# Layer 1's input projection reordered: gate strips ahead of the latents, and the normalised latents kept on chip

## The chip, the cores and the metric

The kernel runs on one NeuronCore of one Trainium2 chip. Five engines work side by side, each through an instruction list of its own that is fixed when the kernel is built: PE (TensorE, matmuls and transposes), DVE (VectorE), ACT (ScalarE), POOL (GpSimd) and SP (SyncE, which here only issues DMAs). They wait for each other through semaphores. The metric is device time in microseconds (us) of one execution. Before the change the median of three executions is 1457.54 us, from 1457.47 to 1457.69.

## The reference, cut to what matters

A two-layer encoder trunk on 1024 tokens of width 1024 in float32. Layer 0 is differential attention, layer 1 multi-head latent attention (MLA), and a last RMSNorm closes it. The change lies in the projections of layer 1:

```python
proj = h @ w_in
q_a, c_kv, k_pe, z = split(proj, [384, 640, 704])         # 384, 256, 64 and 1024 columns
q = (_rmsnorm(q_a, q_a_norm_g) @ w_q_b).reshape(b, s, 8, 192)
q_nope, q_pe = q[..., :128], _rope(q[..., 128:], positions)
k_pe = _rope(k_pe[:, :, None, :], positions)[:, :, 0]
kv = (_rmsnorm(c_kv, kv_a_norm_g) @ w_kv_b).reshape(b, s, 8, 256)
k_nope, v = kv[..., :128], kv[..., 128:]
sc = (einsum('bqhd,bkhd->bhqk', q_nope, k_nope) + einsum('bqhr,bkr->bhqk', q_pe, k_pe)) * 192 ** -0.5
o = einsum('bhqk,bkhd->bqhd', softmax(sc), v)
out = (o * silu(z)) @ w_out
```

So q_a (three strips of 128 columns) and c_kv (two strips) each need an RMS norm over their own columns before anything can be projected out of them. The gate z (eight strips) and k_pe (one) need no norm.

## The kernel before, in words

**Split arithmetic.** Every float32 operand of a matmul is held as two tiles, a rounded high half and a low half (what rounding left over), and each product is three matmuls of 128x128 by 128x512: high·high, high·low, low·high (`mm3`, L177 to L180; the weight's half is named first). A weight tile that a DMA brought to "wraw" is split by ACT (wh, L223) and POOL (wl, L224).

**Strips.** All activations are kept transposed: 128 columns of a projection on the partitions, tokens along the row, in two halves of 512 tokens. A half strip of h takes 8 steps of `mm3`, 24 matmuls. `w_s1` numbers layer 1's strips: 0 is k_pe, 1 to 3 the q latents, 4 and 5 the kv latents, 6 and 7 the gate of head 0 and 1. The gates of heads 2 to 7 are made two at a time by `z_pair` (L1408 to L1435), a Strassen-like scheme: 7 products of 12 matmuls instead of 8 for two strips by two halves. Products 2, 3, 1 and 4 use sums and differences of quarters of h, built on DVE and ACT by `combos` (L1233 to L1260); the weights of a pair are combined on DVE in `z_weights` (L1383 to L1386: zs, then a21, a11 and a12 in their "zraw" tiles), then split. The product with TC[2] is the third of a pair and uses the combination a11 of L1385.

**Norms.** `lora` (L1276) takes a group of latent strips. ACT copies each half strip to "craw" (L1282) and squares it; DVE adds the squares up in "csum" (L1290). When the last strip of the group is through, four matmuls with a column of ones sum over the columns (cps, L1295), DVE and POOL make the inverse root (c_w, L1297; rq_y, L165), and since it is then one number per token lying on the wrong axis, it goes out to DRAM (bc_d, L401) and comes back spread over all partitions (bc_s, L403). DVE scales craw by it (L1304), ACT rounds the high half (c_h, L1308), POOL takes the low one (L1309), and both halves are stored to DRAM in "cS" (L1315, L1316). These steps stand in a list that `run_norms` empties one stage at a time, at the fifth step of a half strip (`NORM_AT = 4`).

**Order of the stage.** Second token half of h is made from x (transposes trh, L482; the scaled copies h1f); strips 0 and 1 for the first half run meanwhile. Then strip 0 and 1 second half, 2, 3, 4, 5, the gates 6 and 7, three `z_pair`s, in the last of which 20 DMAs of 256 KB bring the latents back (`load_ck`, L1458 to L1462). Then eight value tiles of heads 0 to 3 one after the other (`v1_tile`, L1448: 6 matmuls, a split by ACT and DVE at L356, a store of 512 KB to "vS" at L358). Then the stream of q and k strips: strip qr (rope part of two heads), kn and qn of head 0, with the value tiles of heads 4 to 7 set between them by `V1_AT = (3, 2)`: 3 tiles after 6 steps, 2 tiles after the remaining ones of 16, 3 after the first scores. Rope needs its rows swapped, which four DMAs do (rp_sw, L319), a DVE add (rp_r, L329), and DMAs that stack the halves (qpa, L350; qpb, L351).

**What sets the order.** The program text. Loops over matmul steps call `side.tick()`, which runs one entry of a queue of small tasks; the list of each engine follows from the text and from a scheduler that keeps an engine's list in an order by readiness, save where the text pins it (`keep_in_program_order`). SP's list holds every DMA of the stage, loads, stores and norm rows alike, in one queue: a DMA whose data is late holds back those behind it. Tiles come from pools of fixed size ("zraw" 6, "wraw" 2, "u" 20), and a tile's next user waits for its last reader.

## Time and profile before

| what | number |
|---|---|
| median of three executions | 1457.54 us |
| the profiled execution, its own time | 1457.54 us |
| its span in the trace | 1457.5 us |
| PE, matmul instructions | 7388 |
| first half strip of layer 1 begins | about 782 us |
| the three pairs | 898.5 to 957.2 us |
| first scores of layer 1 | 994.96 us |
| DMA traffic of the whole | 213.70 MB |

The span and the execution's own time differ by under 0.1 us, so what is found in the trace can be set against the time as it is. A row of the profile names its line (L1295 is line 1295), its engine, the operation and its tiles (out<-in). In a timeline row the two numbers ahead are the start and the duration in us, and the bracket behind tells how long the engine had been idle and what ended that. A window row gives for each engine the busy time and the number of instructions, then the clock that PE was granted (1.00 is full), the share of the DMA engines that was busy, and what they moved. A PE that waits shows as missing busy time; a PE with a lowered clock shows as busy, but its matmuls are longer.

### The profile page before, as it was taken

The numbers are of one execution on the slowest core, as the hardware profiler recorded it, in microseconds if no ns is written. First come the engines' busy times: TensorE is split into PE (matmuls) and PEld (weight loads), VectorE is DVE, ScalarE is ACT, GpSimd is POOL, SyncE is SP. The second block draws the span as 40 slices with busy tenths as digits, with TensorE's granted clock in tenths as the row PEclk, the third lists the DMA queues.
The fourth block names the chain that finished last, engine by engine and source line by source line (L and its number), as shares of the span: only waits on it lengthen the run. The fifth ranks groups of instructions, "written<-read, shape, count | busy, mean of one in ns | idle before, by whom it ended". The sixth has DMA issues, their size and how long they took to land. (4 is left out here: it accounts for less than half of the span.)

```text
span 1457.5 us, 20649 instructions
## 1 busy us (share of the span) xinstructions
PE 1396.9 (96%) x7388; PEld 1166.4 (80%) x7388; DVE 917.9 (63%) x1362; ACT 727.8 (50%) x1287; POOL 627.6 (43%) x493
## 2 busy tenths in 40 slices
PE   5999999999999999998999879989999999999997
PEld 4778788888888887886787768867888888888886
DVE  6656777767777767687355964544666555555355
ACT  5622365656566665565343433334455554545342
POOL 4416164656465555543641455422141331412572
PEclk9999999999999999999999989999999999999999
DMA  9787723333332424237743145398443432336563
GB/s 329 228 252 237 245 67 99 85 99 87 102 93 82 114 68 117 59 87 261 253 144 123 44 152 173 107 289 211 146 125 123 118 104 65 110 97 215 181 234 141
DMA packets 135527, 213.70 MB, mean 147 GB/s; under 512 B 19072, under 2 KB 56064, under 8 KB 135424
## 3 DMA queue, kind: packets, MB, share of 16 engines
q1 hardware_dynamic: 135424, 212.38, 47.7%
q8 instruction: 58, 0.95, 0.3%
q14 instruction: 45, 0.37, 0.1%
HBM read 137.92 MB, written 50.80 MB: 129 GB/s over the span
## 5 line engine op out<-in xcount | busy, mean ns | idle before, releaser
L378 ACT CAST pth<-tr 128x512 fp32r<-128x512 f32 x256 | 150.3, 587 | 281.7 <-PE tr L376 280.0
L393 DVE TENSOR_REDUCE nm<-s 128x1 f32<-128x1024 f32 x192 | 234.0, 1219 | 76.8 <-PE s L767 65.7
L379 DVE TENSOR_TENSOR ptl<-tr,pth 128x512 fp32r<-128x512 f32 x256 | 176.1, 688 | 140.1 <-ACT pth L378 139.6
L224 POOL TENSOR_TENSOR wl<-wraw,wh 128x512 fp32r<-128x512 f32 (+2 forms) x81 | 106.8, 1321 | 210.7 <-ACT wh L223 202.2
L395 ACT ACTIVATE e<-s,nm 128x1024 f32<-128x1024 f32 x128 | 143.7, 1122 | 31.8 <-DVE nm L393 26.2
L376 PE MATMUL tr<-ident,e 128*128 128x128 f32 x1024 | 154.6, 273 | 2.2 <-DVE ptl L379 1.9
L376 PEld LDWEIGHTS tr<-ident,e 128*128 128x128 f32 x1024 | 121.5, 140 | 42.9 <-DVE ptl L379 19.4
L178 PE MATMUL acc<-h0h,wh 128*128 128x512 f32 x360 | 150.8, 419 | 3.6 <-DVE v_hl L356 3.1
L178 PE MATMUL pv<-pth,vt 128*128 128x256 f32 x512 | 147.2, 287 | 0.0
L179 PE MATMUL pv<-ptl,vt 128*128 128x256 f32 x512 | 145.6, 284 | 0.0
L180 PE MATMUL pv<-pth,vt 128*128 128x256 f32 x512 | 144.6, 282 | 0.0
L180 PE MATMUL acc<-h0h,wl 128*128 128x512 f32 x360 | 142.8, 397 | 0.3 <-POOL wl L224 0.3
L179 PE MATMUL acc<-h0l,wh 128*128 128x512 f32 x360 | 142.1, 395 | 0.0
L1007 POOL TENSOR_TENSOR wol<-wor,woh 128x512 fp32r<-128x512 f32 x64 | 85.6, 1360 | 83.3 <-ACT woh L1006 78.9
L179 PEld LDWEIGHTS pv<-ptl,vt 128*128 128x128 f32 x512 | 97.7, 191 | 2.6
L178 PEld LDWEIGHTS pv<-pth,vt 128*128 128x128 f32 x512 | 97.6, 191 | 2.8 <-ACT pth L378 0.2
L180 PEld LDWEIGHTS pv<-pth,vt 128*128 128x128 f32 x512 | 97.7, 191 | 0.1
L320 POOL TENSOR_TENSOR rp_r<-rp_raw,cosT 128x512 f32<-128x512 f32 x38 | 49.8, 1311 | 94.9 <-ACT rp_raw L315 51.7
L325 POOL TENSOR_TENSOR rp_sw<-rp_sw,sinT 128x512 f32<-128x512 f32 x42 | 55.7, 1326 | 77.8 <-DMA rp_sw<-rp_raw 73.0
L767 PE MATMUL s<-ks,qa 128*128 128x512 f32 x256 | 82.0, 402 | 3.0 <-DVE e L775 2.7
L775 DVE SCALAR_TENSOR_TENSOR e<-s,z,e 128x1024 f32<-128x1024 f32 x64 | 82.1, 1283 | 2.1
L767 PE MATMUL s<-ks,qb 128*128 128x512 f32 x256 | 80.9, 395 | 0.0
(590 smaller groups left out, 3365.2 us busy)
## 6 DMA issues: line engine op xcount, KB each, us to landing
ada<-in_ada_ss SPq DMA_DIRECT2D x32, 512.0 KB, 5.8
wraw<-in_w_s SPq DMA_DIRECT2D x64, 256.0 KB, 2.9
vS<-v_hl SPq DMA_DIRECT2D x32, 512.0 KB, 5.3
vt<-vS SPq DMA_DIRECT2D x32, 512.0 KB, 3.9
wor<-in_w_out SPq DMA_DIRECT2D x64, 256.0 KB, 4.0
rp_sw<-rp_raw SPq DMA_DIRECT2D x168, 64.0 KB, 2.0
bc_s<-bc_d SPq DMA_DIRECT2D x34, 256.0 KB, 4.4
oS<-bc_s SPq DMA_DIRECT2D x30, 256.0 KB, 3.0
```

Of the source, the lines that this page charges most:

```text
L178: PE.matmul(psum, ah, bh, start=first, stop=False)
L179: PE.matmul(psum, ah, bl, start=False, stop=False)
L180: PE.matmul(psum, al, bh, start=False, stop=last)
L224: sub = (V if pair_of else G).tensor_sub(l_[:, :n], raw[:, :n], f32v(h_[:, :n]))
L376: PE.transpose(tr[:, j, :], p[:, kt * P : (kt + 1) * P], ident)
L378: mk["S"] = S.copy(pth[kh][:, :, dst], tr).ins
L379: mk["V"] = V.tensor_sub(ptl[kh][:, :, dst], tr, f32v(pth[kh][:, :, dst])).ins
L393: mk["V"] = V.reduce_max(nm, s_ps, axis=AX.X, negate=True).ins
L395: mk["S"] = S.activation(e, s_ps, AF.Exp, bias=nm, scale=1.0, accum_out=zs).ins
L767: PE.matmul(s_ps[:, kc * HF : (kc + 1) * HF], src[:, c, ql], KS[h][kc][:, c, :], start=fst, stop=not fst)
L775: combined.append(V.scalar_tensor_tensor(out=e0, in0=e1, scalar=z1[:, 0:1], in1=e0, op0=ALU.mult, op1=ALU.add).ins)
L1007: in_turn(G.tensor_sub(lo, raw, f32v(hi)))
```

## The change

The strips are taken in another order. After k_pe come the gates 6 and 7, then the kv latents 4 and 5, then the three pairs; the q latents 1 to 3 come last, as the first three items of the stream that used to begin with qr. The norm of the kv latents runs inside the first pair: `z_pair` calls `late_z`, which now empties one stage of the norm list at each of its three points. The norm of the q latents runs behind the value tiles: eight tiles of heads 0 to 3 are set at every fourth step of the last two q strips and the kn strip (after 16 steps), and those of heads 4 to 7 between kn, qr and qn of head 0 by `V1_AT = ((2, 4), (3, 6), (0, 6), (1, 0))`: number of tiles, then steps of the stream. Two tiles are left for after the first scores.

The normalised latents no longer go to DRAM: cS, its 20 stores and its 20 loads are gone. Their high and low halves go to tiles that stay (pool "ck", 8 tiles, for c_kv, and "u" for q_a). The low half is taken by DVE now (POOL before), in a stage of its own, `split`, one stage behind the scaling.

Smaller edits: the copies of k_pe go from DVE to ACT; the h1f copies of the second token half go from DVE to ACT (`act=gi == 1`); two empty ticks (`G_LATE`) stand ahead of the second half's transposes; the combinations follow each other at 4 ticks (5 before); the value tiles' buffers of layer 1 are 5 (`VB`, 3 before); the size of a scratch area for DMAs is set when the kernel is built.

```diff
-V1_AT = (3, 2)
+QA_V = 16
+V1_AT = ((2, 4), (3, 6), (0, 6), (1, 0))
+G_LATE = 2
-VB = (2, 3)
+VB = (2, 5)
@@ group0
-            h_chunk(1, fulls, k, h1[k][gi], p3x, V, f32=h1f[k] if gi else None)
-        if gi == 0:
-            side.add(*[None] * G_WAIT)
+            h_chunk(1, fulls, k, h1[k][gi], p3x, V, act=gi == 1, f32=h1f[k] if gi else None)
+        side.add(*[None] * (G_LATE if gi else G_WAIT))
...
-            side.add(lambda: w4.append(strip1(0)), None, lambda: w4.append(strip1(1, h1p)))
+            side.add(lambda: w4.append(strip1(0)), None, lambda: w4.append(strip1(6, h1p)))
@@ lora
-            def rest():
+            def scale():
                 for i in range(n):
                     t = craw[i][half]
                     tc.keep_in_program_order(V.scalar_tensor_tensor(
...
-                    hi = pl.tile([P, HF], F32R, name="c_h", tag=tag, bufs=6)
-                    S.copy(hi, t)
-                    G.tensor_sub(t.bitcast(F32R), t, f32v(hi))
-                    his.append(hi)
-                norms.append(store)
-            def store():
-                for i in range(n):
-                    SP.dma_start(cS[dst + i, half, 0], f32v(his[i]))
-                    SP.dma_start(cS[dst + i, half, 1], craw[i][half])
+                norms.append(split)
+            def split():
+                for i in range(n):
+                    t = craw[i][half]
+                    dst[i][half] = hi, lo = part(), part()
+                    S.copy(hi, t)
+                    V.tensor_sub(lo, t, f32v(hi))
...
-    lora((1, 2, 3), 0, qag, QL, w4[1], first_halves)
-    lora((4, 5), 3, kvg, KVL)
-    for h in range(2):
-        w = strip1(6 + h)
+    half_and_norm(w4[0], 1, lambda acc: side.q.insert(8, kp_half(1, acc)))
+    half_and_norm(w4[1], 1, z_put(0, 1))
+    w = strip1(7)
+    for half in range(2):
+        half_and_norm(w, half, z_put(1, half))
+    for i in range(2):
+        w = strip1(4 + i)
+        for half in range(2):
+            half_and_norm(w, half, lambda acc: ckput(i, half, acc))
...
     def late_z(i):
-        if i == 0:
-            load_ck(CK, 3, [(k, half) for half in range(2) for k in range(2)])
-        if i == 2:
-            load_wk(0)
-            load_ck(CQ, 0, [(i, half) for half in range(2) for i in range(3)])
+        run_norms()
-    z_pair(1)
+    z_pair(1, late_z)
     load_wk(1)
-    z_pair(2)
-    z_pair(3, late_z)
-    for tt in range(NT):
-        v1_tile(tt, 0, p4)
+    z_pair(2, late_z)
+    z_pair(3, late_q)
+    cqput = lora(3, CQ, qag, QL, lambda: ut("cqr", dt=F32), lambda: ut("cq"), 1)
...
-    items, steps1 = [], []
+    items = [(lambda i=i: fetch_strip([A["w_s1"][1 + i, f] for f in range(2)], [4, 4]), h1, lambda acc, half, i=i: cqput(i, half, acc)) for i in range(3)]
...
-    stream1.step(6)
+    stream1.step(QA_V)
+    for tt in range(NT):
+        v1_tile(tt, 0, p4)
+        stream1.step(4)
+        if tt % 2:
+            run_norms()
-    for n, steps in zip(V1_AT, (steps1[0] - 6, 0)):
+    for n, steps in V1_AT:
         for tt in v1_left[:n]:
             v1_tile(tt, 1, ap, "pt", 6)
+            run_norms()
         del v1_left[:n]
         stream1.step(steps)
```

**First place: SP in the first pair.** These are consecutive entries of SP's queue. zraw are weights of the next pair, zS gates on their way to DRAM (gz those of heads 0 and 1, z and zu those of a pair). Before:

```order
L1356 DMA zraw<-in_w_s 128x512
L1364 DMA zS<-gz 128x512
L1356 DMA zraw<-in_w_s 128x512 x2
L1395 DMA zS<-z_8758 128x512
L1356 DMA zraw<-in_w_s 128x512
L1395 DMA zS<-z_8822 128x512
L1395 DMA zS<-zu_8803 128x512
L1356 DMA zraw<-in_w_s 128x512
L1395 DMA zS<-zu 128x512
```

After, with the rows of the norm (bc_d out, bc_s back) between them:

```order
L1352 DMA zraw<-in_w_s 128x512 x4
L1386 DMA zS<-z_8430 128x512
L403 DMA bc_d<-rq_y 128x4 x2
L405 DMA bc_s<-bc_d 128x512
L1352 DMA zraw<-in_w_s 128x512
L405 DMA bc_s<-bc_d 128x512
L1386 DMA zS<-z_8522 128x512
L1386 DMA zS<-zu_8488 128x512
L204 DMA wraw<-in_w_s 128x512
L1386 DMA zS<-zu 128x512
```

The two bc_d now stand one behind the other, and the first bc_s behind both. In the kernel before, the norm of the kv latents was over by then.

**Second place: DVE in the first pair**, from the weights zs of the next pair on. L1385 before and L1374 after make a11 in its zraw tile. Before:

```order
L1383 TENSOR_TENSOR zs_8890<-zraw 128x512
L1384 TENSOR_TENSOR zraw<-zraw 128x512
L1422 TENSOR_TENSOR zu_8803<-zacc,zu 128x512
L1426 TENSOR_TENSOR z_8822<-zacc,zu_8803 128x512
L1427 TENSOR_TENSOR zu<-zacc,zu 128x512
L1385 TENSOR_TENSOR zraw<-zs_8890,zraw 128x512
L1394 SCALAR_TENSOR_TENSOR z_8822<-zth,z_8822 128x512
L1432 TENSOR_TENSOR zu_8803<-zacc,zu_8803 128x512
L1386 TENSOR_TENSOR zraw<-zraw 128x512
```

After:

```order
L1418 TENSOR_TENSOR z_8522<-zacc,zu_8488 128x512
L1311 SCALAR_TENSOR_TENSOR craw<-craw,vec,bc_s 128x512 x2
L1419 TENSOR_TENSOR zu<-zacc,zu 128x512
L1385 SCALAR_TENSOR_TENSOR z_8522<-zth,z_8522 128x512
L1320 TENSOR_TENSOR ck<-craw,ck 128x512
L1424 TENSOR_TENSOR zu_8488<-zacc,zu_8488 128x512
L1320 TENSOR_TENSOR ck<-craw,ck 128x512
L1311 SCALAR_TENSOR_TENSOR craw<-craw,vec,bc_s 128x512 x2
L1385 SCALAR_TENSOR_TENSOR zu_8488<-zth,zu_8488 128x512
L1426 TENSOR_TENSOR zu<-zacc,zu 128x512
L1436 CAST wvh<-wvr 128x512
L1374 TENSOR_TENSOR zraw<-zs_8600,zraw 128x512
```

Four scalings (craw, two at a time) and two low halves (ck) stand among the sums of the gates, and the row of a11 now comes behind all but one of the pair's own rows.

**Third place: the way to the first scores.** First DVE. Before, from the last gate row on:

```order
L1394 SCALAR_TENSOR_TENSOR zu<-zth,zu 128x512
L356 TENSOR_TENSOR v_hl<-vps,v_hl 128x512 x11
L1531 TENSOR_TENSOR kn_l<-acc,kn_h 128x512
L329 TENSOR_TENSOR rp_r<-rp_r,rp_sw 128x512
L1531 TENSOR_TENSOR kn_l<-acc,kn_h 128x512
L1539 SCALAR_TENSOR_TENSOR qn_l<-acc,qn_h 128x512
L329 TENSOR_TENSOR rp_r<-rp_r,rp_sw 128x512
L1539 SCALAR_TENSOR_TENSOR qn_l<-acc,qn_h 128x512
L356 TENSOR_TENSOR v_hl<-vps,v_hl 128x512 x2
```

After, from the scaling of the q latents on (cqr the raw strips, cq their low halves):

```order
L1311 SCALAR_TENSOR_TENSOR cqr<-cqr,vec,bc_s 128x512 x3
L1320 TENSOR_TENSOR cq<-cqr,cq 128x512
L1510 TENSOR_TENSOR kn_l<-acc,kn_h 128x512
L1320 TENSOR_TENSOR cq<-cqr,cq 128x512
L358 TENSOR_TENSOR v_hl<-vps,v_hl 128x512
L1320 TENSOR_TENSOR cq<-cqr,cq 128x512
L1311 SCALAR_TENSOR_TENSOR cqr<-cqr,vec,bc_s 128x512 x3
L1320 TENSOR_TENSOR cq<-cqr,cq 128x512
L358 TENSOR_TENSOR v_hl<-vps,v_hl 128x512
L1320 TENSOR_TENSOR cq<-cqr,cq 128x512
L358 TENSOR_TENSOR v_hl<-vps,v_hl 128x512
L1320 TENSOR_TENSOR cq<-cqr,cq 128x512
```

The scalings and low halves of the q latents stand between the low halves of kn and those of the value tiles. Now SP. Before, from the eight value stores of heads 0 to 3 on:

```order
L358 DMA vS_0_71<-v_hl 256x4x128 x8
L202 DMA wraw<-in_w_kn 128x256
L319 DMA rp_sw<-rp_raw 32x512 x4
L202 DMA wraw<-in_w_qn 128x384
L319 DMA rp_sw<-rp_raw 32x512 x4
L350 DMA qpa<-qpa 64x512
L351 DMA qpa<-qpa 64x512
L350 DMA qpb<-qpb 64x512
L351 DMA qpb<-qpb 64x512
L358 DMA vS_1_72<-v_hl 256x4x128 x3
L350 DMA qpa<-qpa 64x512
L351 DMA qpa<-qpa 64x512
```

After, from the first norm row of the q latents on:

```order
L405 DMA bc_s<-bc_d 128x512
L360 DMA vS_1_72<-v_hl 256x4x128
L403 DMA bc_d<-rq_y 128x4
L360 DMA vS_1_72<-v_hl 256x4x128
L204 DMA wraw<-in_w_kn 128x256
L405 DMA bc_s<-bc_d 128x512
L369 DMA vt<-vS_0_71 128x1024
L360 DMA vS_1_72<-v_hl 256x4x128
L321 DMA rp_sw<-rp_raw 32x512 x3
L360 DMA vS_1_72<-v_hl 256x4x128 x2
L321 DMA rp_sw<-rp_raw 32x512 x5
L360 DMA vS_1_72<-v_hl 256x4x128
```

The eight value stores no longer stand in one block; the norm rows, the next weights (wraw), the loads of values (vt) and the stores of the second value half share the stretch, and the rope's swapped rows (rp_sw) stand among the stores.

More of the change, by code (lines that the diff above doesn't have):

```diff
@@ L1280, in put @@
         def put(i, half, acc):
[L1281 removed]
+            t = raw()
             S.copy(t, acc)
@@ L1290, in put @@
                 V.tensor_add(sums[half], sums[half], s2)
+            if i == n - 1:
+                f = lambda: norm(half)
+                for _ in range(lag):
+                    f = lambda f=f: norms.append(f)
+                norms.append(f)
         def norm(half):
@@ L1318, in norm @@
-            his = []
-            norms.append(rest)
-        for i, si in enumerate(idx):
-            w = strip1(si) if i or ws is None else ws
-            for half in range(2):
-                if (i, half) == (0, 0) and first:
-                    first(lambda acc: put(0, 0, acc))
-                else:
-                    half_and_norm(w, half, lambda acc: put(i, half, acc))
-                if i == n - 1:
-                    norms.append(lambda half=half: norm(half))
-    def first_halves(put):
-        nonlocal p4
-        g0 = kp_half(0, strip_half(w4[0], h1, 0))
-        for _ in gen_half(w4[1], h1, 0, put):
-            side.tick()
-        side.flush()
-        st3x.close()
-        p4 = pool(st4, "p4")
-        g0()
-        cg = combos()
-        for _ in range(16):
-            side.add(None, None, lambda: next(cg), None, None)
-        accs = []
-        for _ in gen_half(w4[0], h1, 1, accs.append):
-            side.tick()
-        kp_half(1, accs[0])()
@@ new lines, in z_put @@
+    def z_put(h, half):
+        return lambda acc: SP.dma_start(zS[h, half], silu_gate(wp, acc))
+    g0 = kp_half(0, strip_half(w4[0], h1, 0))
+    for _ in gen_half(w4[1], h1, 0, z_put(0, 0)):
+        side.tick()
+    side.flush()
+    st3x.close()
+    p4 = pool(st4, "p4")
+    cg = combos()
+    side.add(None, g0)
+    for i in range(16):
+        side.add(None, None, lambda: next(cg), None)
+    half_and_norm(w4[0], 1, lambda acc: side.q.insert(8, kp_half(1, acc)))
+    half_and_norm(w4[1], 1, z_put(0, 1))
```

81 lines of the change are left out of this document (38 added, 43 removed).

## The prediction, as put on record before the changed kernel ran

> **What bounds the kernel now.** I read the page's busy shares first, then PE by windows over layer 1's projection, then who PE waits for there, then the timeline at those waits. On the page PE is busy for 96% of the span, so nothing but PE time, waits of PE or its clock, can move the end:
>
> ```profile
> span 1457.5 us, 20649 instructions
> PE 1396.9 (96%) x7388; PEld 1166.4 (80%) x7388; DVE 917.9 (63%) x1362; ACT 727.8 (50%) x1287; POOL 627.6 (43%) x493
> ```
>
> The windows (length; busy us of PE, PEld, DVE, ACT, POOL; granted clock; DMA share; GB/s) show where in this stage PE is missing:
>
> ```profile
> 780.00:800.00 20.00, 18.50 (x88) 14.39 (x87) 12.70 (x20) 11.26 (x17) 3.85 (x3) 1.00 0.33 119
> ...
> 820.00:840.00 20.00, 15.51 (x62) 12.22 (x61) 17.08 (x24) 8.25 (x16) 5.63 (x5) 0.88 0.15 40
> 840.00:860.00 20.00, 20.00 (x87) 16.24 (x87) 12.94 (x11) 7.88 (x15) 12.94 (x8) 0.94 0.47 145
> 860.00:880.00 20.00, 12.66 (x50) 10.35 (x48) 11.85 (x15) 6.51 (x13) 7.99 (x6) 0.74 0.58 184
> 960.00:980.00 20.00, 16.22 (x71) 12.76 (x69) 6.13 (x9) 5.96 (x11) 1.29 (x1) 1.00 1.00 305
> 980.00:1000.00 20.00, 17.08 (x57) 12.73 (x58) 7.03 (x10) 7.01 (x13) 10.62 (x9) 0.83 0.62 164
> ...
> 870.00:875.00 5.00, 5.00 (x16) 4.23 (x17) 1.54 (x3) 0.00 (x0) 2.62 (x2) 0.50 0.20 58
> ```
>
> Idle PE: 1.50 + 4.49 + 7.34 + 3.78 + 2.92 = 20.0 us. The clock takes a second toll. It falls to half after a gap (0.50 at 870 to 875). Time lost to it is the missing clock: (0.12 + 0.06) x 20 = 3.6 around the first norm, 0.26 x 20 = 5.2 around the second, of which I strike 1.7 as falling in idle time anyway, and 0.17 x 20 = 3.4 at the first scores; 10.5 us. Together 30.5 us. The waits behind it (us in total, times, longest):
>
> ```profile
> PE cps L1295 <- DVE csum L1290: 11.8, 2, 7.3
> PE acc L178 <- ACT wh L223: 3.6, 1, 3.6
> PE s L1587 <- DVE qn_l L1539: 1.9, 1, 1.9
> PE trh L482 <- DVE xfull L471: 1.5, 2, 0.8
> PE acc L178 <- DVE v_hl L356: 0.7, 1, 0.7
> PE acc L180 <- POOL wl L224: 0.4, 1, 0.4
> ```
>
> The two cps waits are the norm sums of q and of kv: PE reaches the column sums in its list while DVE and ACT are still deep in the combinations, so the last square is added late. The 3.6 is the kn weight, behind the value stores on SP:
>
> ```profile
> 869.54 1.84 PE L1295 MATMUL cps<-ones,csum 128*128 128x1 f32 x8 [7.34 <-DVE csum L1290]
> 960.56 15.42 SPq L358 DMA_DIRECT2D vS<-v_hl  x8
> 976.08 0.66 SPq L202 DMA_DIRECT2D wraw<-in_w_kn  x1
> 980.51 0.50 PE L178 MATMUL acc<-ckh,wh 128*128 128x512 f32 x1 [3.55 <-ACT wh L223]
> ```
>
> **What the change takes away.** All of that. While the combinations run, PE now has gate strips, which need no norm; a gate costs ACT one tanh and DVE one multiply, and nothing on PE waits for them. The column sums of kv stand in the first pair, more than one product after the last square. The eight value stores are strewn among q strips, and kn's weight is fetched ahead of them; 40 transfers of 256 KB vanish. So -30.5 us: 1427.0, if nothing new waits. PE's own work is what it was: the same matmuls in another order. POOL gives DVE ten low halves (about 0.7 us each, 7 us), DVE gives ACT eight h1f copies: beside PE both are free as long as the engines keep ahead, which is what the next part asks. At the start the second half's transposes come two ticks later; by the order PE still reaches them 0.8 us before DVE's scaled x; I keep 0.8 of the 1.5.
>
> **New wait A, the second pair.** One product of a pair takes 2.8 us (starts 904.3, 907.1, 909.8 below):
>
> ```profile
> L178 PE MATMUL zacc<-t2h,wh x12: 388/389/395, 904.3 to 945.0; 128*128 128x512 f32 x12
> L178 PE MATMUL zacc<-t3h,wh x12: 389/389/389, 907.1 to 947.8; 128*128 128x512 f32 x12
> L178 PE MATMUL zacc<-t1h,wh x12: 389/389/389, 909.8 to 950.5; 128*128 128x512 f32 x12
> ```
>
> From the start of pair 1: the first sums at 8.4 to 9.2, TC[3] to 12.0, the second sums to 12.8, and the rest of the pair to 21.2; pair 2 then reaches its third product, on a11, at 26.8. SP sends the second bc_d ahead of the first bc_s, so the scaling of the first half waits for the second sums too. Rows for the steps:
>
> ```profile
> 836.56 1.01 POOL L165 TENSOR_TENSOR rq_y<-c_w,mhalf 128x4 f32<-128x4 f32 x1 [0.70 <-DVE c_w L1297]
> L1304 DVE SCALAR_TENSOR_TENSOR craw<-craw,vec,bc_s x10: 1133/1144/2192, 845.6 to 889.7; 128x512 f32<-128x512 f32 x10
> DMA to landing us min/median/max: 3.0/4.3/5.9
> 912.73 0.69 DVE L1426 TENSOR_TENSOR z<-zacc,zu 128x512 f32<-128x512 f32 x1 [1.45 <-PE zacc L180]
> 914.58 0.69 DVE L1385 TENSOR_TENSOR zraw<-zs,zraw 128x512 f32<-128x512 f32 x1 [0.56 <-POOL wl L224]
> 920.89 0.62 ACT L223 CAST wh<-zraw 128x512 fp32r<-128x512 f32 x1 [0.96 <-PE zacc L179]
> 921.58 1.29 POOL L224 TENSOR_TENSOR wl<-zraw,wh 128x512 fp32r<-128x512 f32 x1 [1.50 <-ACT wh L223]
> ```
>
> (The landing row is that of bc_s around the norms of before.) DVE's c_w and POOL's root (1.01) end at 14.1, SP issues the second bc_d and then bc_s at 14.5, and bc_s lands 4.3 later, at 18.8. From there the order has, ahead of a11, four scalings (1.14 each), three sums, two gate rows, two low halves and the cast of wvh (0.69 each): 4.6 + 5.5 = 10.1. So DVE begins a11 at 28.9 and has it at 29.6, ACT's cast (0.62) gives wh at 30.2, and POOL's low half (1.29) is there at 31.5, where PE, two matmuls of 0.23 on, would want it at 30.7. PE stands from 26.8 to 30.2 and another 0.8: 4.2 us. Before, the same row began at 914.58, two products and a half ahead of the matmul that uses it (the row t2 above, second pair: about 923.7). Bounds: 2 if bc_s lands in 3.0 and the gate rows slip ahead of the scalings' wait; 6 if two scalings meet other traffic (1.14 against 2.19 in the row above). The same stall takes clock: one window at half clock, about 3.4 us long, costs 1.7 us. A is 5.9. Were a11 set ahead of the scalings, nothing would be left of it: its inputs (L1372, L1373) stand ahead of even the second c_w in DVE's list.
>
> **New wait B, q's norm.** From PE's end of the last q strip, in the same units: sums at 0.8, root and bc_d; SP has a weight load that waits for POOL and a load of values ahead of bc_s, which goes out at about 4.1 and lands at 8.4 to 10. DVE then has three scalings, three low halves, a kn half and a value tile: 3.4 + 5 x 0.69 and its waits for ACT's casts, to 14.8. The second bc_s stands on SP behind the load of the next kn weight, which needs a wraw tile back, and lands near 13.3; three more scalings to 18.1, low halves at 18.7, 19.9 and 21.1, with value tiles between. PE's cover is value tiles and kn until 11.4; qr and qn then take 36 matmuls to 19.8 if nothing waits, and by these times they end at 22.5. That is 2.7 us; I take 3.5, since DMA will be busier than I can count (bounds 2.7 and 5). The wait comes in pieces of about 1 us, and I give it no clock.
>
> **New wait C, the first scores.** qr's rope now comes late, and its swaps share SP with value stores:
>
> ```profile
> rp_sw<-rp_raw SPq DMA_DIRECT2D x168, 64.0 KB, 2.0
> vS<-v_hl SPq DMA_DIRECT2D x32, 512.0 KB, 5.3
> qpa<-qpa SPq DMA_DIRECT2D x16, 128.0 KB, 2.3
> L393 DVE TENSOR_REDUCE nm<-s 128x1 f32<-128x1024 f32 x192 | 234.0, 1219 | 76.8 <-PE s L767 65.7
> L395 ACT ACTIVATE e<-s,nm 128x1024 f32<-128x1024 f32 x128 | 143.7, 1122 | 31.8 <-DVE nm L393 26.2
> 990.00:995.00 5.00, 3.13 (x15) 2.28 (x13) 2.18 (x4) 2.76 (x6) 3.39 (x4) 1.00 0.81 212
> 995.00:1000.00 5.00, 5.00 (x15) 3.98 (x16) 2.18 (x3) 0.14 (x1) 0.60 (x1) 0.66 0.95 269
> ```
>
> In B's units, SP has the last swap of qr's first half behind two value stores, and DVE its add behind the seventh value tile, at 26.5; ACT's copies, POOL's low halves and two landings of 2.3 bring qpa at 30.8 and qpb at 32.8. PE's cover (values, kn, kn of the next head) lasts till 31 to 33: a close fit, and I cost it at nothing; without that cover it is up to 2. With two tiles (2.8 us) instead of three behind the first score, the maximum (1.22) and the exponentials (1.12) are not covered: 2.1 us idle. The two rows above show what such a short gap does: 1.87 us idle, and the clock is 0.66 in the next 5 us, 1.7 us lost. C is 3.8.
>
> **The sum.** 1457.5 - 30.5 + 0.8 + 5.9 + 3.5 + 3.8 = 1441.0. The profiled execution is the median, 1457.54, so nothing is to be shifted.
>
> **Rivals.** *Short gaps cost no clock*: without the 1.7 us in A and in C, 1437.6. For it: 1.50 us missing at 780 to 800 left the clock at 1.00. Against: the 1.87 us above. The Trainium skill, "TensorE: Matmul & The Clock Gate", section "🎯 Why this matters for your kernels", says to avoid gaps over about 3 us, since one idle window brings the lower clock; by that rule 1.87 us should have been free, which the row at 995 contradicts, and the time would be the rival's.
>
> *The order hides all three* (DVE runs earlier rows than I reckon, bc_s lands in 3): 1427.0 + 0.8, and some 2 us of small waits: 1430. For it: DVE is busy only 6 to 7 of 20 us at 960 to 1000; against: A needs ten DVE rows to shrink, and each of the three chains is counted from rows of the same work.
>
> *The new waits eat most of it*: A at 6 with two half-clock windows (9.4), B at 5 with one (6.7), C doubled (7.6): 23.7 + 0.8, 1451.5; 1449 to 1454.
>
> *Slower: SP's queue.* The eight stores held SP for 15.4 us. If q's bc_d comes to stand behind such a backlog, the norm arrives 15.4 us late, with qr and qn behind it and all cover used up: 15.4 plus three half-clock windows (5.1), over the 14.0 of the sum: 34.5 against 30.5 gained, 1461.5. It decides from a backlog of 14.3 us on (14.0 + 5.1 + 14.3 = 33.4, 0.2% over what is gained). Against: the stores are 3 us or more apart now, where each took 1.9, and DMA loses 10 MB of traffic.
>
> *No change in effect*: gain and new waits even out within 0.2%, which is about what a measurement of this kernel can tell (2.9 us): new waits of 27.6 to 33.4 are needed.
>
> **Chances.** Forecast 0.50 (own range 1436 to 1446), no clock cost 0.12, all hidden 0.16, most eaten 0.12, even 0.05, slower 0.05. Faster by over 0.2% is the first four, 0.90; within 0.2% 0.05; slower 0.05. The range leaves out the slower and even cases and the far ends of the two beside the forecast, about 2 in 10: 1429 to 1451.
>
> **What the profile after must show.** No cps wait on csum above 1 us, clock 1.00 through the combinations, no vS block of 15 us on SP: else the 30.5 is wrong. PE waiting at the third product of pair 2 for wh or wl made from a11 (L1374): A. A wait of qr or qn on DVE's low halves of cq (L1320): B. A wait of tr on e after the first score, and the clock falling: C. If A is absent, DVE made a11 ahead of the scalings' wait, and I have read the list too literally; if cps still waits, the latents' squares are again behind the combinations. DVE should grow by only about what POOL loses less the h1f copies; a stretch of DVE at 20 of 20 with PE waiting would mean the low halves were not free.

## The result, and the profile after

Five executions of the changed kernel took 1448.94 to 1453.26 us, median 1452.22; five of the kernel before took 1457.47 to 1463.44, median 1457.69. The ratio is 0.9942, with a 95% interval from 0.9924 to 0.9961: 8.4 us less (5.7 to 11.1). The prediction said 16.5 us less. Half of the gain is missing.

One number of the baseline has to be put right first. In every later execution of either kernel the own time is 1.7 to 1.9 us above the span (for the kernel before, 1459.84 with a span of 1458.0); only the first three executions, with 1457.54 beside a span of 1457.5, show no such distance, and no run says why. So spans are set against spans here: the forecast of 1441.0 is one, and the five of the changed kernel are 1447.2 to 1451.5, median 1450.4. That is 7.1 us below 1457.5, inside the range of 1429 to 1451 and outside the forecast's own 1436 to 1446. The profiled execution, 1447.2, is the shortest of the five. Own times give the same picture: in the runs below, 43 more executions of the kernel before took 1459.7 on average, and the five of the changed kernel 1451.65, 8.0 us less.

The page of the changed kernel, the same two rows as of before:

```profile
span 1447.2 us, 20558 instructions
PE 1392.7 (96%) x7388; PEld 1161.4 (80%) x7388; DVE 913.5 (63%) x1360; ACT 733.6 (51%) x1299; POOL 609.6 (42%) x483
```

The matmuls are as many as before. PE's idle time fell from 60.6 to 54.5 us, and its busy time by 4.2, which with the same matmuls is clock. Window by window (the columns as in the prediction):

```profile
820.00:840.00 20.00, 18.49 (x78) 14.36 (x79) 19.71 (x26) 10.77 (x20) 6.72 (x5) 1.00 0.42 122
840.00:860.00 20.00, 20.00 (x96) 16.52 (x95) 9.28 (x14) 6.45 (x11) 10.70 (x9) 1.00 0.34 91
860.00:880.00 20.00, 15.26 (x57) 11.48 (x56) 17.73 (x21) 7.37 (x13) 11.80 (x7) 0.83 0.36 105
...
960.00:980.00 20.00, 15.40 (x49) 10.54 (x48) 14.27 (x18) 7.08 (x13) 2.01 (x2) 0.83 0.75 190
980.00:1000.00 20.00, 16.22 (x67) 12.93 (x66) 8.29 (x11) 9.43 (x16) 8.98 (x7) 0.92 0.59 151
```

Through the combinations (820 to 860) PE is busy and the clock full, where it lost 4.49 us and clock before. But 15.4 us of idle time are left in the stage (0.8 + 1.5 + 4.7 + 4.6 + 3.8), against 20.0 before and 10.6 forecast. The waits of PE name where:

```profile
PE tr L378 <- ACT e L397: 3.8, 1, 3.8
PE zacc L182 <- POOL wl L226: 2.4, 1, 2.4
PE zacc L180 <- ACT wh L225: 2.3, 1, 2.3
PE acc L181 <- DVE cq L1320: 2.2, 3, 1.6
PE acc L180 <- ACT cq L1319: 2.2, 1, 2.2
PE acc L182 <- POOL wl L226: 1.5, 2, 0.9
PE trh L484 <- DVE xfull L473: 0.8, 1, 0.8
```

No cps waits for csum any more, and no weight waits behind the value stores. The two zacc rows are the prediction's A, the cq rows B, the first row C. The 1.5 us for wl at 820 to 840 (a kv strip's weights) were not foreseen.

**A.** The third product of pair 2, from timelines of PE, DVE and POOL:

```profile
859.67 2.19 DVE L1311 SCALAR_TENSOR_TENSOR craw<-craw,vec,bc_s 128x512 f32<-128x512 f32 x2 [1.70 <-DMA bc_s<-bc_d]
869.26 0.67 DVE L1374 TENSOR_TENSOR zraw<-zs,zraw 128x512 f32<-128x512 f32 x1
869.48 3.39 POOL L1437 TENSOR_TENSOR wvl<-wvr,wvh 128x512 fp32r<-128x512 f32 x1 [6.15 <-DVE wvh L1436]
870.71 0.79 PE L180 MATMUL zacc<-t2h,wh 128*128 128x512 f32 x1 [2.33 <-ACT wh L225]
872.84 3.13 POOL L226 TENSOR_TENSOR wl<-zraw,wh 128x512 fp32r<-128x512 f32 x2
874.33 0.79 PE L182 MATMUL zacc<-t2h,wl 128*128 128x512 f32 x1 [2.40 <-POOL wl L226]
```

With the start of pair 1 at 841.4 (the product was wanted at 868.2, which is 26.8 later), the scaling began at 18.3 (forecast 18.8) and a11 at 27.9 (28.9). PE stood for 4.73 us (4.2), but in other shares: 2.33 for wh instead of 3.4, 2.40 for wl instead of 0.8. POOL took up that wl only at 872.84, behind the low half of a value weight (wvl, 3.39 us), which the prediction's sum does not have.

**B.** SP on the way to q's norm, with the landing times of the two bc_d and the two bc_s there, and DVE's scaling of the second half:

```profile
957.87 0.33 SPq L405 DMA_DIRECT2D bc_s<-bc_d  x1
...
958.98 0.82 SPq L403 DMA_DIRECT2D bc_d<-rq_y  x1
...
966.08 0.32 SPq L405 DMA_DIRECT2D bc_s<-bc_d  x1
DMA to landing us min/median/max: 3.0/4.4/7.1
970.28 4.30 DVE L1311 SCALAR_TENSOR_TENSOR cqr<-cqr,vec,bc_s 128x512 f32<-128x512 f32 x3 [1.51 <-DMA bc_s<-bc_d]
```

The second bc_s left at 966.08 because the 2 KB of its bc_d, issued at 958.98, took 7.1 us to land. In the kernel before the median was 1.4, by its list of DMAs:

```profile
bc_d<-rq_y SPq DMA_DIRECT2D x19, 2.0 KB, 1.4
```

Beside the row in the same queue stood value stores and value loads of 512 KB. In the prediction's units (the last q strip ends at about 952.6) the first row landed at 9.9, where 8.4 to 10 was forecast, and the second at 17.6 instead of 13.3. PE waited for cq for 4.45 us, forecast 3.5.

**C.** The last rows ahead of the first transposes, on ACT, DVE and PE:

```profile
993.11 1.07 ACT L1509 CAST kn_h<-acc 128x512 fp32r<-128x512 f32 x2
993.73 0.69 DVE L1510 TENSOR_TENSOR kn_l<-acc,kn_h 128x512 fp32r<-128x512 f32 x1 [1.94 <-ACT kn_h L1509]
994.33 2.35 DVE L395 TENSOR_REDUCE nm<-s 128x1 f32<-128x1024 f32 x2
996.84 1.03 PE L378 MATMUL tr<-ident,e 128*128 128x128 f32 x4 [3.78 <-ACT e L397]
```

PE had finished the scores at 992.8. DVE did not take their maximum: the low half of the next head's kn stood ahead of it in DVE's list, its high half stood on ACT behind the casts of qpa's second half, and the maximum began at 994.33, 1.5 us late. That is most of the 1.7 us by which C (3.78) exceeds the forecast (2.1).

### The profile page after: what moved, and what is told of

Read it like the earlier page. It is cut to its first block, busy times and chain, and to the rows that moved or that the text cites. A ratio compares the mean times of both kernels' runs of the same rounds, so it can differ in the third digit from the quotient of the medians.

```text
span 1447.2 us, 20558 instructions
## 1 busy us (share of the span) xinstructions
PE 1392.7 (96%) x7388; PEld 1161.4 (80%) x7388; DVE 913.5 (63%) x1360; ACT 733.6 (51%) x1299; POOL 609.6 (42%) x483
## 4 chain that ended last, share of the span: by engine, by line
PE 78%; DMA 7%; DVE 6%; issue 3%; ACT 2%; POOL 2%; SPq 1%; ACTq 0%; POOLq 0%; DVEq 0%
PE s L1567 10%; PE acc L182 8%; PE acc L181 8%; PE acc L180 8%; PE tr L378 7%; PE s L769 7%; PE pv L180 4%; PE pv L181 4%; PE pv L182 4%; PE oacc L181 3%; PE oacc L180 3%; PE oacc L182 3%; DMA wvr<-in_w_v 1%; PE zacc L182 1%; DMA ada<-in_ada_ss 1%
```

## The experiments

All edits are to the changed kernel, except where another base is named. "Own time" is the median of the runs timed beside runs of the kernel before on the same chip (median 1459.3 to 1459.8 there). The changed kernel was not timed again beside them: its five executions above (mean 1451.65, ratio 0.9942 with some 0.002 either way) are what the runs are compared with, so a difference of less than 3 to 4 us from it is not clear of noise.

**1. kv's norm one stage earlier**

```diff
-    ckput = lora(2, CK, kvg, KVL, lambda: pv1.tile([P, HF], F32, name="craw", tag="wv1", bufs=4), lambda: ckp.tile([P, HF], F32R, name="ck", tag="ck", bufs=8), 1)
+    ckput = lora(2, CK, kvg, KVL, lambda: pv1.tile([P, HF], F32, name="craw", tag="wv1", bufs=4), lambda: ckp.tile([P, HF], F32R, name="ck", tag="ck", bufs=8), 0)
```

> The changed kernel with kv's norm one stage earlier (lag 0 in place of 1), so that its scalings stand before the DVE rows of the first pair. The changed kernel has 2.33 + 2.40 us of PE waiting at the third product of pair 2, for wh and wl of a11. Theory (the norm's scalings, held by the norm row, keep DVE from a11): both waits fall, together below 1 us, the clock at 865 to 880 stays above 0.95, span some 6 us below 1447.2, about 1441. Rival 1 (POOL's own queue, the low half of the value weight ahead of wl, makes the stall): the wait for wl stays at 2 us or more, span 1444 or above. Rival 2 (an earlier sum meets late squares, as in the kernel before): a new wait of cps for csum of 1 to 3 us, span 1443 to 1446.

Own time 1451.31, ratio 0.9947 (0.9932 to 0.9962), span of the profiled run 1447.2: no gain. Waits of PE:

```profile
PE cps L1302 <- DVE csum L1292: 2.5, 1, 2.5
...
PE zacc L182 <- POOL wl L226: 1.4, 1, 1.4
```

The 4.73 us of A are gone, so the norm's place in DVE's list made them. In exchange the first column sum meets a late square again (2.5 us, and the clock is 0.83 at 840 to 860), and a wait for wl of 1.4 appears at another product. The theory was right on the cause. Rival 2 was right on the new wait; its span of 1443 to 1446 was too short.

**2. One more stage of the norm list after the seventh value tile**

```diff
-        if tt % 2:
+        if tt % 2 or tt == 6:
             run_norms()
```

> The changed kernel with one more stage of the norm list run, after the seventh value tile: q's first norm starts 2.8 us earlier and its first row goes out ahead of two weight loads. The changed kernel has 4.45 us of waits for cq (1.57 + 0.23 in the first half, 2.22 + 0.43 in the second). Theory (SP's order and the late start of the norm are the cause): they fall to 1.5 us or less, the half clock at 975 to 980 goes, span 4 to 6 us below 1447.2. Rival (DVE is the bound there, 14.3 of 20 us busy at 960 to 980): the scalings only move, the waits stay above 3 us, span within 2 us of 1447.2. A wait of cps for csum above 1 us would be a third way, span 1446.

Own time 1447.69, ratio 0.9926 (0.9909 to 0.9942), span 1444.7. From the waits of PE and the timeline of DVE:

```profile
PE acc L180 <- ACT cq L1319: 6.0, 1, 6.0
965.79 0.16 DVE L1304 TENSOR_SCALAR c_w<-cps 128x4 f32<-128x4 f32 x1
976.58 3.25 DVE L1311 SCALAR_TENSOR_TENSOR cqr<-cqr,vec,bc_s 128x512 f32<-128x512 f32 x3 [5.84 <-DMA bc_s<-bc_d]
```

This is 4 us below the changed kernel by own times and 2 by the ratios, whose intervals overlap. The first half's waits for cq vanished, the second half's grew to 6.0: its c_w, a row of 0.16 us, now stood on DVE behind the first half's scaling, which waited for its row until 961.43. C was gone, since the maximum, at 992.39, now stood ahead of kn in DVE's list, and the next head's kn matmuls stood behind the scores on PE and covered it (from 993.35 on). One gap of 6.0 in place of several of 1.6 to 3.8: B grew by 1.5 and C's 3.8 went. The stated theory fell (no fall to 1.5 us, and a span 2.5 us shorter instead of 4 to 6). The waits stayed above 3 us as the rival had it, but not for its reason: DVE was not full, it stood idle for 5.84 us until the row came.

**3. Three value tiles left for after the first scores**

```diff
-V1_AT = ((2, 4), (3, 6), (0, 6), (1, 0))
+V1_AT = ((2, 4), (2, 6), (0, 6), (1, 0))
```

> The changed kernel with two value tiles instead of three between kn and qr, so that three instead of two are left for after the first scores. The changed kernel has PE idle for 3.78 us before the first transposes, waiting for the exponentials. Theory (the maximum stood behind a low half of kn on DVE, 994.33 instead of about 992.4, and two tiles do not cover maximum and exponentials): the wait falls to 1 us or less, and what one tile less of cover costs ahead of the scores is up to 1.4 us more waiting for cq or qpa; span 1 to 4 us below 1447.2. Rival (the rope's swapped rows set the start of the scores, whatever covers it): the wait for the exponentials falls, and a wait of s for qpa or qpb of as much takes its place; span within 1 us of 1447.2.

Own time 1449.59, ratio 0.9936 (0.9921 to 0.9951). No wait for the exponentials was left, so C is what was said. But the waits for cq rose from 4.45 to 6.3 us, and 1.1 us for a value tile's low half came:

```profile
PE acc L180 <- ACT cq L1319: 4.3, 2, 3.6
PE acc L181 <- DVE cq L1320: 2.0, 3, 1.6
```

The tile that was moved had been cover for B: 1.85 us of C's 3.78 came back there. The span of the profiled execution, 1449.7, is not the 1 to 4 us below 1447.2 that the theory gave, and the own time is 2.1 us below the changed kernel's mean, which is within noise. No wait of s for qpa appeared; the rope was not the rival.

**4. The kernel before with the scratch setting**

```diff
-num_devices=1)
+num_devices=1, dynamic_dma_scratch_size=1024)
```

> The kernel before with the scratch area for DMAs set to 1024 as in the change, and nothing else. The changed kernel's own time lies 1.74 us over its span (1448.94 and 1447.2) in every run, where the kernel before had 0.0. Theory (the scratch setting costs nothing inside the span, and is what adds 1.7 us outside it): span 1457.5, own time 1459.2. Rival (the 1.7 us come from the rest of the change, or from the way of counting): own time 1457.5.

Own time 1460.67, ratio 1.0004 (0.9993 to 1.0015), own time 1.8 above the span. The runs of the unchanged kernel beside it show the same 1.8 us. The setting costs nothing that can be measured, and the 1.7 us are not its doing. That leaves the way of counting, which the rival named, as the likely source; no run shows it, and the rival's time of 1457.5 was not seen again.

**5. Without the row's way through DRAM**

```diff
-            _, rb = bcast_rows(wp, y, "rp", 6)
+            rb = t3(cosT[:, 0:HF])
```

> The changed kernel without the way of the norm row through DRAM: DVE scales the latents by a row of the rope table that lies on chip (so the latents' norm is left out of the result); sums, c_w and the root are still made, bc_d and bc_s are not. Theory (A and B both come from the row's way: SP's order, the landing of bc_d and bc_s, and DVE held by it): the waits at the third product of pair 2 (4.73 us) and for cq (4.45 us) fall below 1.5 us together, C stays (3.8 us), span 9 to 14 us below 1447.2: 1433 to 1438. Rival (DVE and ACT are what is short there: scalings, low halves and casts are the same in number): at least half of A and B, 4.5 us or more, stays, span 1441 or above.

Own time 1437.56, ratio 0.9839 (0.9822 to 0.9855): 14 us below the changed kernel. Four waits of PE are left in the stage. Two, 1.5 us for wl and 0.8 for xfull, are as in the changed kernel; the others are:

```profile
PE tr L378 <- ACT e L397: 4.5, 1, 4.5
...
PE acc L181 <- DVE cq L1320: 0.6, 1, 0.6
```

A is zero, B 0.6, with all scalings, low halves and casts still there in number. So A and B are in the main the row's journey and not a want of DVE or ACT. The edit changed one thing more: a scaling from the table takes DVE 0.74 us for the q latents where one from bc_s took 1.14, and 0.82 instead of 1.13 in the median for the kv latents. That is at most 1.6 us over the four scalings of A and 1.2 over three of B, so a part of this size is not shown to be the journey's. 8.6 us of waiting less went with 14 us of time. Some 5 us of the rest is clock: of the stage's windows of 20 us only 980 to 1000 is below full here (0.83), where 0.83, 0.83 and 0.92 stood.

**6. The second value weights split after pair 2**

```diff
-    load_wk(1)
     z_pair(2, late_z)
+    load_wk(1)
```

> The changed kernel with the split of the second value weights (cast on DVE, low half on POOL) after pair 2 instead of before it. In the changed kernel POOL worked at the low half of the value weight from 869.48 to 872.87, ahead of wl of a11, and PE waited 2.40 us for that wl after 2.33 us for wh. Theory (A has two parts, DVE's list for wh and POOL's list for wl; the prediction gave the second 0.8 us): the wait for wl falls to 1 us or less, that for wh stays at 2.0 to 2.5 less the one cast, span 1.5 to 3 us below 1447.2. Rival (wl is late since wh is, and POOL's slow rows come from DVE's traffic beside it): the wait for wl stays above 2 us, span within 1 us.

Own time 1449.91, ratio 0.9931 (0.9914 to 0.9948), against 0.9942: no difference that can be told. The wait for wl stayed at 2.08 us, though POOL had stood idle for 7.40 us before:

```profile
873.79 4.16 POOL L226 TENSOR_TENSOR wl<-zraw,wh 128x512 fp32r<-128x512 f32 x2 [7.40 <-ACT wh L225]
876.58 0.80 PE L182 MATMUL zacc<-t2h,wl 128*128 128x512 f32 x1 [2.08 <-POOL wl L226]
```

Two low halves took 4.16 us, where one takes 1.29 when POOL is alone. From a11's row on DVE ran without a break; while POOL was at the first of the two, a12's row and a low half stood there:

```profile
871.97 0.68 DVE L1374 TENSOR_TENSOR zraw<-zs,zraw 128x512 f32<-128x512 f32 x1
...
873.77 0.69 DVE L1375 TENSOR_TENSOR zraw<-zraw 128x512 f32<-128x512 f32 x1
874.38 0.69 DVE L1320 TENSOR_TENSOR ck<-craw,ck 128x512 fp32r<-128x512 f32 x1
```

The theory (POOL's list) fell and the rival held: in the changed kernel wl did stand behind wvl, but with wvl out of the way wl itself is as slow. That DVE's work beside it is the reason rests on these rows alone; no run took it away. The Trainium skill, "SBUF — State Buffer", section "🔬 SBUF: two separate sides", says that a DVE instruction with two operands in SBUF and a GpSimd instruction that reads SBUF exclude each other for their whole length; that fits these rows, in which the two DVE rows end at 875.07 and the wl that PE waits for is there 1.5 us later, at 876.58.

**7. q's norm earlier, with the second half's sums ahead of the first half's scaling**

```diff
-        if tt % 2:
+        if tt % 2 or tt == 6:
...
-                    f = lambda f=f: norms.append(f)
-                norms.append(f)
+                    f = lambda f=f: norms.insert(0, f)
+                norms.insert(0, f)
...
-            norms.append(scale)
+            norms.append((lambda: norms.append(scale)) if n == 3 and half == 0 else scale)
```

> As the run with one more stage of the norm list after the seventh value tile, but with the second half's sums and c_w ahead of the first half's scaling, which stood on DVE between them there (c_w ended at 965.9, the second row landed at 976.6, a wait of 6.0 us for cq). Theory (the second row was late because its c_w was queued on DVE behind a scaling that waits for the first row): the 6.0 us fall to 2 us or less, C stays gone or below 1 us, span 1438 to 1441. Rival (2 KB of bc_d behind value stores and value loads in the DMA queues set it, 7.1 us to landing in the changed kernel): bc_d of the second half again takes 5 us or more, the wait for cq stays at 3 us or more, span 1443 or above.

Own time 1453.51, ratio 0.9953 (0.9938 to 0.9968). The wait for cq fell to 2.8, bc_d took 1.7 and some 2.6 us to land here, but bc_s 5.4 and 6.2; and C came back larger, since both low halves of kn stood ahead of the maximum again:

```profile
PE tr L378 <- ACT e L397: 4.9, 1, 4.9
```

A also came out longer (3.0 + 3.1), though the rows of kv's norm leave in the same order as before. The edit did what it was to do on the norm, and the time did not follow. Run 2 is 4 (by the ratios) to 6 us faster: there C is absent, where it is 4.9 here, and A is 1.3 shorter, against 3.2 more for cq.

**8. Edits 6 and 7, and kv's norm earlier but at the eighth step of a half strip**

```diff
-NORM_AT = 4
+NORM_AT = 7
```

> The last two edits together, and kv's norm a stage earlier, but run at the eighth step of a half strip instead of the fifth, so that the first sum does not meet a late square (2.5 us of cps waiting for csum at the fifth step). Theory: no wait at the third product of pair 2 above 0.5 us, cps for csum below 1 us, the rest as in the run before: span 1431 to 1436, own time 1.8 more. Rival (DVE is full in the combinations, 19.8 of 20 us busy at 820 to 840, so any earlier norm step delays them or waits for them): 2 us or more of waits for csum or for a combination appear, span 1437 or above.

Own time 1452.16, ratio 0.9945 (0.9930 to 0.9959). A is gone, but the column sum still waited 3.0 us for csum, so three steps more did not help: the rival held. C was 4.9, cq 2.6. The waits of the stage have moved, and the time is the changed kernel's.

**9. The row spread on chip**

```diff
-            _, rb = bcast_rows(wp, y, "rp", 6)
             def scale():
+                dg, row = rpt("dgs"), bank("m", "rb")
+                for j in range(4):
+                    js = slice(j * P, (j + 1) * P)
+                    V.tensor_scalar(dg[:, js], ident, y[:, j : j + 1], None, op0=ALU.mult)
+                    PE.matmul(row[:, js], ones, dg[:, js], start=True, stop=True)
+                rb = t3(row)
```

> The changed kernel with the norm row spread over the partitions on chip, as the kernel already does at the end of a layer: DVE multiplies the identity by the four columns of the root (0.28 us each), PE multiplies a square of ones by that (4 matmuls of 0.275), DVE scales from the result. PE gets 4 x 1.1 = 4.4 us of work more, DVE 4.5. Theory (the row's way through DRAM costs the changed kernel 14 us, as the run without it showed: own time 1437.6 against 1451.6): own time 1437.6 + 4.4 = 1442, range 1440 to 1446; no DMA wait for bc_s, wait for cq and at the third product of pair 2 together below 2 us; C stays (4.5 us). Rival (the four matmuls stand on PE where their data is late): a new wait of PE for dgs of 2 us or more, own time 1447 or above.

Own time 1441.19, ratio 0.9877 (0.9854 to 0.9899): 18 us less than the kernel before, and within 1 us of the expectation. A and B are gone, so the theory held there; C, which was to stay at 4.5, is 2.4. The matmuls wait a little for their data, less than the rival's 2 us:

```profile
PE tr L378 <- ACT e L397: 2.4, 1, 2.4
PE rb L1311 <- DVE dgs L1310: 1.6, 2, 1.0
```

As in run 5 the scalings are shorter as well, 0.74 us each instead of 1.13 to 1.15.

**10. Run 9 with three value tiles left** (V1_AT as in run 3)

> The run before with three value tiles left for after the first scores. Theory (C is the maximum behind kn's low half on DVE, and too few tiles; with the norm row on chip there is no late cq that the missing tile had covered): the wait for the exponentials (3.8 to 4.9 us in all runs with two tiles left) falls below 1 us and no wait takes its place, own time 4 to 6 us below the run before, about 1437. Rival (one tile less ahead of the scores uncovers qpa): a wait of s for qpa or qpb of 2 us or more, own time within 2 us of the run before.

Own time 1439.44, ratio 0.9871 (0.9850 to 0.9891), the fastest version that computes the whole result, 19 us below the kernel before. C is gone; a wait of 2.0 us for a value tile's low half came in its place:

```profile
PE vps L180 <- DVE v_hl L358: 2.0, 1, 2.0
```

Against run 9 the means of four runs differ by 1.7 us and the intervals overlap: the theory was right on C and wrong on the 4 to 6 us.

**11. The first eight value tiles in one block behind the q strips**

```diff
-    stream1.step(QA_V)
+    stream1.step(QA_V + 32)
     for tt in range(NT):
         v1_tile(tt, 0, p4)
-        stream1.step(4)
```

> The changed kernel with the eight value tiles of heads 0 to 3 behind the q strips in one block, as in the kernel before, so that q's norm has 11.2 us of PE work more as cover, and bc_d stands on SP behind four value stores. Theory (what makes q's norm late is the queue of value stores, on SP and in the DMA engines): bc_d and bc_s each take 5 us or more to land, the stores hold SP for 12 us or more, and in spite of the cover PE waits 2 us or more for cq or for the rope's rows; own time within 3 us of the changed kernel's 1451.6. Rival (the distance between norm and use is all that matters): no wait for cq, C as before, own time 1446 or less.

Own time 1453.88, ratio 0.9962 (0.9948 to 0.9976). With 11 us more of cover PE still stood 6.9 us in one piece, not for cq but for room: an accumulator of kn could not be freed, its low half standing on DVE behind six scalings that waited for the row.

```profile
PE vps L180 <- DVE kn_l L1510: 6.9, 1, 6.9
967.08 6.86 DVE L1311 SCALAR_TENSOR_TENSOR cqr<-cqr,vec,bc_s 128x512 f32<-128x512 f32 x6 [4.19 <-DMA bc_s<-bc_d]
951.62 5.72 SPq L360 DMA_DIRECT2D vS<-v_hl  x4
957.38 2.02 SPq L403 DMA_DIRECT2D bc_d<-rq_y  x2
```

bc_d and bc_s each took 4.4 to 5.2 us to land behind the stores. The stores ahead of the rows held SP for 5.7 us, not for 12. The time is as the theory had it; the wait that took the place was another.

**12. The h1f copies on DVE again**

```diff
-            h_chunk(1, fulls, k, h1[k][gi], p3x, V, act=gi == 1, f32=h1f[k] if gi else None)
+            h_chunk(1, fulls, k, h1[k][gi], p3x, V, f32=h1f[k] if gi else None)
```

> The changed kernel with the eight h1f copies of the second token half on DVE again (0.8 us each, 6.4 us), as in the kernel before. Theory (the reordering, not this edit, freed PE in the combinations: the first pair needs them only 5 us or more after DVE has done them): PE waits no more at 780 to 860 than the 2.3 us of the changed kernel plus 1, own time within 2 us of 1451.6. Rival (DVE, 19.8 of 20 us busy at 820 to 840, has no room for 6.4 us more): waits of 3 us or more for wl or for a combination at 820 to 860, own time 1455 or above.

Own time 1454.18, ratio 0.9963 (0.9950 to 0.9976), some 3 us above the changed kernel, with intervals that overlap. The waits at 780 to 860 are 2.9 us in place of 2.3, with one gap of 1.63 after which the clock fell (0.95 and 0.96 in the two windows), A 5.3. The theory's waits held (2.9, where at most 3.3 was allowed) and its time did not; the rival's waits for wl did not come. What the edit is worth stays open between 0 and some 5 us.

## Why the prediction was half right

**The 30.5 us removed: right on the waits.** All six named waits are gone except 0.8 of the 1.5 at xfull, as said. Runs 1 and 8 show the cause as read: bring the sum back into the combinations, and 2.5 to 3.0 us of csum return.

**A, B and C: each was there, at its named place.** A was 4.73 of idle time against 4.2, B 4.45 against 3.5, C 3.78 against 2.1. Runs 1 and 5 confirm the cause of A, run 5 that of B. For C the named cause was one value tile too few; runs 3 and 10 confirm that a third tile covers it, but in run 2 two tiles were enough, with the maximum ahead of kn in DVE's list. So the order around the maximum makes C as much as the number of tiles, and the prediction did not look at it.

**The mis-sized terms.** Idle time: 15.4 in place of 10.6. Of these 4.8 us, C has 1.7 (the maximum stood behind the low half of the next head's kn, which was not costed; the order shown for the third place ends before it), the weights of the kv strips 1.5 (not foreseen; ACT casts wh among the combinations' casts), B 0.95 (the second row landed 4.3 us later than forecast: the prediction had its bc_s wait for the load of the next kn weight, and it waited for its own bc_d, 7.1 us to landing), A 0.5 (wl behind wvl on POOL, and POOL's rows beside DVE's). Clock: B was given none, since the wait was taken to come in pieces of 1 us. One piece was 1.57 us, at 964.86, and left the clock at full; another was 2.22 us, at 970.94, and the windows after it run at half:

```profile
967.00:970.00 3.00, 2.77 (x11) 1.67 (x10) 1.77 (x3) 0.41 (x1) 0.00 (x0) 1.00 0.91 190
...
973.00:976.00 3.00, 2.41 (x5) 1.50 (x6) 3.00 (x5) 1.82 (x4) 0.00 (x0) 0.51 0.01 2
976.00:980.00 4.00, 4.00 (x11) 3.11 (x10) 2.18 (x4) 0.00 (x0) 0.00 (x0) 0.51 0.72 201
```

By the windows of 20 us the clock cost 0.17 x 20 + 0.17 x 20 + 0.08 x 20 = 8.4 us, of which about 2.4, worked out in windows of 5 us, fall in idle time: 6.0 against 3.4. Together 4.8 + 2.6 = 7.4 us more than the sum had. The profiled execution, from which these numbers are, lies 6.2 us above the forecast (1447.2 against 1441.0), so some 1.2 us were gained outside the stage or by chance. The median execution is 3.2 us longer still; no trace shows where.

**The rivals.** *No clock cost* fell: A, the longer gap of B and C were each followed by a half-clock stretch. *All hidden* fell. *The new waits eat most of it* came nearest: every wait went towards its upper end, and its 1449 to 1454 holds the median span of 1450.4, which the forecast's own 1436 to 1446 does not. It had been given 0.12. That the whole range still holds the median span is owed to its width, and the profiled 1447.2 alone would flatter the forecast. *SP's queue* fell as a whole, but a mild form of it is in B: a norm row among value stores. In run 11 the rows stand behind four stores, and even there the kernel stays faster than before.

**Where the gain went, then:** into the row's way through DRAM. It used to lie under the next strips' matmuls; at its new places its 5.9 to 11.3 us, from the issue of bc_d to the landing of bc_s, do not fit under one pair or under a few value tiles, and DVE, which takes its list in order, holds the rest back with it. Run 5 puts its cost at up to 14 us here (with the shorter scalings in that number), and run 9 shows that some 4.4 us of PE work in its place leave a gain of 10.

## What to carry to other kernels

When a step with a long journey (sums, a root, out to DRAM and back) is moved behind less work, cost the journey from its worst row in the trace, and look at what stands behind its first user on an in-order engine, since that is late too. Shifting such a step by hand moved waits to other places in runs 1, 2, 3, 7 and 8, and only run 2 came out shorter, by 2 to 4 us, which is not clear of noise; making the journey short, even for some PE time, took the waits away and 10 us with them. And cost a gap on PE of about 2 us or more with its clock: taking 8.6 us of waits away in run 5 came with some 5 us less lost to it.

## What the runs showed that was not expected

- **The clock and short gaps.** Gaps of 1.87 (before), 2.22 (after) and 2.37 us (run 9) were followed by a stretch at about half clock, and one of 1.98 us (run 10) by a clock of 0.67 in the next 3 us. So were gaps of 1.63 and 1.56 us in run 12 and one of 1.36 us in run 1. Gaps of 1.57 us (after), 1.59 (run 4) and 0.97 (run 9) were not, and not even one of 2.94 us in run 11. The windows behind the 1.63 of run 12, behind the 1.36 of run 1, and around the end of the 2.94 of run 11 with PE's row there:

```profile
838.00:841.00 3.00, 3.00 (x7) 2.43 (x8) 2.93 (x4) 1.48 (x3) 1.58 (x1) 0.52 0.28 87
...
969.50:973.00 3.50, 3.50 (x9) 2.50 (x9) 1.86 (x3) 0.93 (x2) 1.15 (x1) 0.51 0.89 309
...
1003.74 0.44 PE L378 MATMUL tr<-ident,e 128*128 128x128 f32 x2 [2.94 <-ACT e L397]
1003.00:1006.00 3.00, 2.26 (x12) 1.96 (x13) 1.25 (x2) 2.30 (x5) 1.04 (x1) 1.00 0.66 146
```

  So the length of a gap alone does not decide it in these runs: from some 1.4 us on a gap can cost clock, and one of 2.94 us need not. Where the prediction set one row against the rule of the Trainium skill, "TensorE: Matmul & The Clock Gate", section "🎯 Why this matters for your kernels" (no gaps over about 3 us), seven gaps under 3 us that cost clock now stand.
- **A 2 KB row can take 7.1 us to land.** 1.4 us is the median of bc_d over the kernel before. The second bc_d of q's norm took 7.1 (after), 6.7, 7.1 and 7.2 in runs 1, 3 and 6, where it was issued 0.7 us after a value store of 512 KB in the same queue; 4.3 in run 2, 1.8 us after one; and some 2.6 in run 7, 4.7 us after one. Run 11, with four stores right ahead, has 5.2 and 4.6. That the stores are what delays it fits these numbers; no run took them away.
- **POOL beside DVE.** A low half takes POOL 1.29 us alone, 3.39 (after) and about 2.8 (run 6) beside DVE rows that read two operands on chip. An engine that is 42% busy can still be the one that is waited for.
- **Executions of one kernel differ more than the first three runs showed.** Those lay within 0.2 us; over all runs the kernel before took 1454.87 to 1464.08, and the mean granted clock of these executions lay between 0.987 and 0.992, lowest in the longest ones. A profile of one execution carries some us of luck: the changed kernel's was 2.7 us below the mean of its five.
